# Two hybrid blocks in float32: twenty pairs of projections by seven block products, with accumulating DMAs for weight sums

## Chip, cores and metric

The kernel runs on one core of a Trainium2 chip. The metric is the device time of one execution in microseconds; a faster kernel has a smaller time. All times here are of the kernel before unless the text says otherwise.

## What is computed

Two blocks follow each other on 512 tokens of width 2048, all in float32. Each normalises its input, projects it, mixes tokens in two ways side by side, gates each mix with a silu of a projection, and projects back onto the residual. The first block puts 16 meta tokens in front (528 in all). Cut to what the change touches:

```python
hn = rmsnorm(h, pre_norm_g[layer])                      # 528 x 2048
proj = jnp.einsum('bld,dc->blc', hn, w_in[layer])
qa, ka, va, ga, qb, kb, vb, gb = jnp.split(proj, SPLIT_POINTS, axis=-1)
ya = gqa_axial_mixer(qa, ka, va, ...) * jax.nn.silu(ga)  # 8 heads of 128, 2 key heads
yb = diff_attn_mixer(qb, kb, vb, ...) * jax.nn.silu(gb)  # 8 heads, two softmaxes each
y = jnp.einsum('blc,cd->bld', jnp.concatenate([ya, yb], axis=-1), w_out[layer])
h = h + rmsnorm(y, post_norm_g[layer])
```

The second block (a gated linear recurrence beside stick-breaking attention) stays as it was.

## The kernel before

**Precision.** Every large matmul is done in halves of float32 that TensorE takes at full pace. `split` (L147) makes them: ScalarE copies a tile into its rounded half, and VectorE subtracts that from the original for the rest. Three products (hi-hi, hi-lo, lo-hi; `PASSES`, L282) then give the float32 result, so each block of 128 x 128 weights costs three matmuls per stretch of tokens. The first block's input x, scaled by g1, lies split in `big` for all 16 K tiles; the factor of the row norm is applied to the results.

**Weights.** `_sequence` (L77) lists all weight units in order; each has two halves of 128 x 1024. `load_next` (L257) issues a half's DMA on SP's queue into one of three raw buffers (`wraw`) and splits it into one of three split buffers (`wsp`). `take` (L273) keeps two halves ahead of TensorE.

**Main work.** `main_work` (L931) does the first block's projections in this order: KA, VA, QA0, the A gates (GA 0 to 7), QA1, the B gates (GB 0 to 7), then for each B head QB, KB, VB, then the output projection O1. `fm` (L284) makes one unit of 128 output columns: 16 K tiles x three passes, with the weights stationary and tokens moving. Gates and QB need the 512 real tokens only (one matmul of 512 columns), KB and VB need all 528 (two of 264, half the tokens each, with a load of the weights in front of each). A gate is finished by `silu2` (L430) into `ybuf`; QB, KB, VB into `qs_`, `ks_`, `vs_` in `ar`.

**Side work.** Attention heads are generators beside the main one: `a_scores`, `a_sums`, `b_scores`, `b_values`, `b_sums`. An A head normalises and rotates its queries (`rope`, L444, on VectorE and GpSimd), then for four query tiles makes scores in PSUM (`pss`), their maximum on VectorE (L622), the exponential on ScalarE (L624) and a scaling by the reciprocal sum on VectorE (L627). `pv_steps` (L480) transposes the weights, splits them (`pt`) and multiplies by the values; `gate_y` (L437) multiplies by the gate in `ybuf`. A B head makes two sets of scores per query tile (L684, L687), scales one (L699) and adds them (L700).

**Order.** `run` (L206) is a planner at build time. It keeps a clock of estimated TensorE time, adds a cost for every matmul (`mm`, L178), and takes the first generator whose posted due times (`post`, L188) have come: sides first, main otherwise. The resulting order is fixed on TensorE; the other engines and the DMA queue of SP follow it too, each strictly in its own order.

Of the kernel before, what the change touches and what calls it, by code (L numbers as in the profile page):

```python
# [40 lines left out]

def _units():
# [6 lines left out]
    for name, n in (("KA", 2), ("VA", 2), ("GA", 8), ("QB", 8), ("KB", 8), ("VB", 8), ("GB", 8)):  # L49
        for i in range(n):  # L50
            u[(name, i)] = ("fm", 0, i, cols)
            cols += P
# [23 lines left out]

def _sequence():  # L77
# [19 lines left out]
def hybrid_two_block_kernel(ctx: ExitStack, tc: tile.TileContext, wp, xT, xtok, par, lvec, cst, rg, pg, lruw, out):  # L97
# [34 lines left out]
    def et(n=L):  # L132
        return T([P, L], "e", F32, 5)[:, :n]
# [98 lines left out]
    ybuf = T([P, KT, NTOK], "ybuf")  # L232
    yflat = flat(ybuf)
# [12 lines left out]
    h1d = dram.tile([NTOK, D], F32, tag="h1d", name="h1d")  # L246

# [7 lines left out]
    loaded = []  # L255

    def load_next(n=1024):  # L257
# [4 lines left out]
        raw = T([P, 1024], "wraw", F32, 3)  # L262
        w = T([P, 2, 1024], "wsp", F32R, 3)
# [7 lines left out]
    taken = [0]  # L271

    def take(unit, h):  # L273
# [3 lines left out]
        while len(loaded) < min(len(seq), i + 1 + AHEAD):  # L277
            for _ in load_next():
                pass
        return loaded[i]  # L280

# [15 lines left out]
    def fm_two(units, ps, lag):  # L297

        w = [None, None]
        for i in range(KT + lag):  # L300
            for u, kt in ((0, i), (1, i - lag)):
                if 0 <= kt < KT:
                    if kt % 8 == 0:
                        w[u] = take(units[u], kt // 8)
# [15 lines left out]
    def tm(units, x0, evac, kgs=range(4), toks=range(NT), before_unit=None, after_unit=None, chore=None):  # L320
# [4 lines left out]
        for i, unit in enumerate(units):  # L325
# [5 lines left out]
            if last:  # L331
                ws_ = [take(unit, 0), take(unit, 1)]
# [80 lines left out]
    kvraw = [ar[:, i * L : (i + 1) * L] for i in range(4)]  # L413
# [7 lines left out]
    qs_, ks_, vs_ = ar[:, 4608:5120], ar[:, 5120:5648], ar[:, 2560:3088]  # L421
    osb, osq, orr = ar[:, 3088:3600], ar[:, 3600:4112], ar[:, 1824:2336]
# [18 lines left out]
    def split_y(s):  # L441
        split(big[:, 0, s, :NTOK], big[:, 1, s, :NTOK], ybuf[:, s, :])

# [36 lines left out]
    def pv_steps(h, tag, e, cols, vt, vs, use, extra=()):  # L480

        for hf in range(2):
            yield when("pt", "ptt", (tag, h, 2 * hf))
            hold("pt")
            pt = T([P, 2, 4, 256], "pt", F32R)
# [37 lines left out]
    def side_norms():  # L523
# [3 lines left out]
        for j in range(5):  # L527
# [3 lines left out]
            xs = yflat[:n, (j % 2) * 2048 : (j % 2) * 2048 + 2048]  # L531
            nc.sync.dma_start(xs, xtok[j * P : j * P + n, :])
            act.activation(yflat[:n, 4096:6144], xs, AF.Square, accum_out=ss0[:n, j : j + 1])
# [711 lines left out]
```

## Time and profile before

| | |
|---|---|
| time, three runs | 1728.32, 1728.72, 1729.15 us (median 1728.72) |
| the profiled execution's own time | 1727.61 us |
| its span, first to last instruction | 1725.8 us |
| granted TensorE clock | 1.0 of full speed |
| TensorE busy | 1714.7 us (99%) |
| VectorE, ScalarE, GpSimd busy | 1015.9, 783.8, 91.0 us |
| first gate to last VB, roughly | 107 to 797 us, without QA1 at 229 to 276 |

The profile is of one execution. Its rows name line, engine and operation, then what is written and read. `pj` is the PSUM of the main work, `pss` that of scores, `pmt` and `ptt` that of the sums and transposes; `wraw` and `wsp` are a weight half raw and split, `e` the score tiles, `ar` a shared area of SBUF. L181 is the matmul helper and L149 and L148 are the two steps of `split`, so for these the tile tells which work it is. Matmuls overlap, so the mean of a single one is longer than their spacing.

### The profile page before, as it was taken

The numbers are of one execution on the slowest core, as the hardware profiler recorded it, in microseconds if no ns is written. First come the engines' busy times: TensorE is split into PE (matmuls) and PEld (weight loads), VectorE is DVE, ScalarE is ACT, GpSimd is POOL, SyncE is SP. The second block draws the span as 40 slices with busy tenths as digits, with TensorE's granted clock in tenths as the row PEclk, the third lists the DMA queues.
The fourth block names the chain that finished last, engine by engine and source line by source line (L and its number), as shares of the span: only waits on it lengthen the run. The fifth ranks groups of instructions, "written<-read, shape, count | busy, mean of one in ns | idle before, by whom it ended". The sixth has DMA issues, their size and how long they took to land.

```text
span 1725.8 us, 23791 instructions
## 1 busy us (share of the span) xinstructions
PE 1714.7 (99%) x9496; PEld 1477.6 (86%) x9496; DVE 1015.9 (59%) x1694; ACT 783.8 (45%) x1276; POOL 91.0 (5%) x85
## 2 busy tenths in 40 slices
PE   8999999999999999999999999999999999999998
PEld 8888888889999999988788998888888888888887
DVE  5748634864566666775557869743223664575433
ACT  6434423443445555564445547822223664575311
POOL 0100001100001101000000001100000000010000
PEclk9999999999999999999999999999999999999999
DMA  8321122222221222222567653222222212432223
GB/s 314 121 98 62 63 84 86 68 79 74 76 84 64 72 74 74 74 69 78 171 196 270 218 190 109 92 94 90 98 98 90 81 61 88 153 115 74 86 97 123
DMA packets 53854, 185.81 MB, mean 108 GB/s; under 512 B 6112, under 2 KB 7776, under 8 KB 52064
## 3 DMA queue, kind: packets, MB, share of 16 engines
q1 hardware_dynamic: 53744, 184.30, 32.2%
q8 instruction: 74, 1.21, 0.3%
q14 instruction: 36, 0.29, 0.1%
HBM read 175.89 MB, written 8.39 MB: 107 GB/s over the span
## 4 chain that ended last, share of the span: by engine, by line
PE 96%; DVE 2%; issue 0%; DMA 0%; POOL 0%; ACT 0%; SPq 0%; DVEq 0%; ACTq 0%; POOLq 0%
PE pj L181 84%; PE pmt L181 4%; PE pss L181 4%; PE ptt L184 2%; PE pmt L184 1%; PE bank L181 1%; PE pss L184 1%; DVE wsp L149 0%; DMA wraw<-in_wp 0%; POOL ybuf L450 0%; SPq L374 0%; ACT wsp L148 0%; POOL ar L450 0%; SPq L266 0%; DVE sm L574 0%
## 5 line engine op out<-in xcount | busy, mean ns | idle before, releaser
L181 PE MATMUL pj<-big,wsp 128*128 128x264 f32 (+2 forms) x4608 | 809.0, 332 | 5.9 <-ACT big L375 5.3
L181 PEld LDWEIGHTS pj<-big,wsp 128*128 128x128 f32 x4608 | 688.2, 189 | 86.9 <-ACT big L375 5.6
L181 PE MATMUL pj<-wsp,big 128*128 128x512 f32 x3072 | 736.5, 396 | 0.6 <-DVE big L149 0.6
L181 PEld LDWEIGHTS pj<-wsp,big 128*128 128x128 f32 x3072 | 569.6, 188 | 131.3 <-DVE big L149 0.9
L149 DVE TENSOR_TENSOR wsp<-wraw,wsp 128x1024 fp32r<-128x1024 f32 (+1 forms) x299 | 363.1, 1215 | 387.1 <-ACT wsp L148 386.7
L148 ACT CAST wsp<-wraw 128x1024 fp32r<-128x1024 f32 (+1 forms) x299 | 310.8, 1040 | 496.0 <-PE pj L181 391.6
L148 ACT CAST pt<-ptt 128x512 fp32r<-128x512 f32 (+2 forms) x96 | 50.3, 524 | 76.1 <-PE ptt L184 76.1
L687 ACT ACTIVATE e<-e,sm 128x528 f32<-128x528 f32 x64 | 47.2, 737 | 77.6 <-DVE sm L684 77.1
L149 DVE TENSOR_TENSOR pt<-ptt,pt 128x512 fp32r<-128x512 f32 (+2 forms) x96 | 59.4, 619 | 35.4 <-ACT pt L148 34.7
L181 PEld LDWEIGHTS pmt<-pt,vv 128*128 128x128 f32 x528 | 69.1, 190 | 3.6
L181 PE MATMUL pss<-kk,qq 128*128 128x264 f32 x448 | 71.4, 287 | 0.0
L181 PE MATMUL pmt<-pt,vv 128*128 128x256 f32 (+1 forms) x528 | 69.6, 280 | 0.0
L181 PEld LDWEIGHTS pss<-kk,qq 128*128 128x128 f32 x448 | 63.5, 188 | 3.7
L684 DVE CUSTOM_DVE_ANT_0 e<-pss,ar 128x528 f32<-128x528 f32 x64 | 45.0, 703 | 31.4 <-PE pss L181 30.9
L184 PE MATMUL ptt<-ident,e 128*128 128x128 f32 x336 | 52.6, 273 | 0.1
L184 PEld LDWEIGHTS ptt<-ident,e 128*128 128x128 f32 x336 | 40.6, 140 | 6.9 <-DVE e L627 0.5
L432 DVE TENSOR_TENSOR e<-pj,rbc 128x512 f32<-128x512 f32 x32 | 22.0, 688 | 39.7 <-PE pj L181 39.7
L885 POOL TENSOR_SCALAR_AFFINE_SELECT e<-e 128x128 f32<-128x128 f32 x32 | 15.7, 490 | 476.2 <-ACT e L884 471.1
L654 POOL TENSOR_SCALAR ar<-ar 128x912 f32<-128x912 f32 x8 | 23.4, 2930 | 211.9 <-DVE sm L684 207.4
L624 ACT ACTIVATE e<-pss,sm 128x528 f32<-128x528 f32 x32 | 22.4, 701 | 23.5 <-DVE sm L622 23.4
L450 POOL TENSOR_TENSOR ar<-ar 128x256 f32<-128x256 f32 x16 | 18.4, 1172 | 242.9 <-DVE ar L447 242.9
L894 ACT ACTIVATE e<-e 128x128 f32<-128x128 f32 (+3 forms) x32 | 15.0, 470 | 28.8 <-DVE e L893 28.5
(202 smaller groups left out, 1168.9 us busy)
## 6 DMA issues: line engine op xcount, KB each, us to landing
wraw<-in_wp SPq DMA_DIRECT2D x295, 512.0 KB, 3.5
e<-in_xT SPq DMA_DIRECT2D x16, 264.0 KB, 4.4
ybuf<-in_xtok SPq DMA_DIRECT2D x4, 1024.0 KB, 7.2
ar<-in_xtok SPq DMA_DIRECT2D x4, 1024.0 KB, 5.9
h1d<-ybuf SPq DMA_DIRECT2D x4, 1024.0 KB, 5.4
ybuf<-h1d SPq DMA_DIRECT2D x12, 256.0 KB, 3.6
out<-ybuf SPq DMA_DIRECT2D x12, 256.0 KB, 2.1
ar<-in_pg SPq DMA_DIRECT2D x1, 1024.0 KB, 4.8
```

The source lines that it names most:

```text
L148: act.copy(hi, src)
L149: dve.tensor_tensor(lo, src, f(hi), ALU.subtract)
L181: _queue(nc.tensor.matmul(out, lhsT, rhs, start=start, stop=stop).ins, cost)
L184: _queue(nc.tensor.transpose(out, in_, identity).ins, 110.0)
L432: dve.tensor_tensor(g, g_ps, rb, ALU.mult)
L450: pool.tensor_tensor(v4(blocks(u))[:, :, :, a, :], v4(x)[:, :, :, 1 - a, :], v4(blocks(s))[:, :, :, a, :], ALU.mult)
L624: act.activation(halves(x), sv, AF.Exp, bias=nm, accum_out=l[:, 0:1])
L654: pool.tensor_scalar(bias, dist, 2.0 ** (-(h + 1)), None, op0=ALU.mult)
L684: dve.tensor_tensor_reduce(out=halves(x), in0=s[:, :, :HL], in1=halves(bias[:, b0 : b0 + L]), scale=1.0, scalar=3e38, op0=ALU.add, op1=ALU ...
L687: act.activation(x, x, AF.Exp, scale=-1.0, bias=nm, accum_out=l[:, m : m + 1])
L885: pool.affine_select(z[:, t * P : w], z[:, t * P : w], [[-1, P]], ALU.is_gt, -1e30, base=0, channel_multiplier=1)
L894: act.activation(c, c, AF.Exp)
```

## The change

It touches the 40 units GA, GB, QB, KB, VB of the first block. They are made in 20 pairs (GA with GA, GB with GB, QB with KB of a head, VB of two heads). For the first 12 of the 16 K tiles, a pair is a 2 x 2 block product: two units by two halves of six K tiles, times two halves of six K tiles by two halves of 264 tokens. It is done with seven block products in place of eight; the last four K tiles are done plainly (`rest`) and accumulate into the same four PSUM banks.

- `seven` is a pair's order on TensorE; `produce(p, i)` is the split of the i-th weight operand, called at fixed places, some for the next pair. Operands 1 to 5, 7 and 9 have 768 columns, 6 and 8 (the plain K tiles) 512.
- Of the four sums of weight blocks, the first is done by VectorE (r0 + r1), the other three by DMAs issued on GpSimd that add from DRAM into SBUF (`sum_up`).
- The sums of x blocks are made once (`side_x`); one of them replaces a quarter of `big`.
- `p1s`, `us`, `wv`, `ts` hold parts of the combination, which ScalarE copies or VectorE makes out of PSUM; the `evac_` functions finish the blocks.
- `ybuf` gives its room to the x sums during this stage. So gates are stored to DRAM (`gated`), loaded again before their head's sum, and the results are stored (`yd`) and loaded again before O1 (`fetch_y`). QA1's result goes through DRAM too (`qd`).
- The order becomes KA, VA0, QA0, QA1, VA1, the gate pairs, then QB/KB, VB/VB, QB/KB for two heads at a time. O1's weights aren't prefetched before the last pair is done (`barred`).
- `e` has six buffers instead of five, and the scalings of L627 and L699 go to ScalarE.

The diff, cut to its core (the removed loop over QB, KB, VB and the function `gate` stand in the code above; posts and unchanged uses of renamed areas are left out):

```diff
+def _pairs():
+    pairs = [(("GA", i), ("GA", i + 1)) for i in range(0, 8, 2)] + [(("GB", i), ("GB", i + 1)) for i in range(0, 8, 2)]
+    for h in range(0, 8, 2):
+        pairs += [(("QB", h), ("KB", h)), (("VB", h), ("VB", h + 1)), (("QB", h + 1), ("KB", h + 1))]
+    return pairs
+
...
-    seq = [("VA", 0), ("VA", 1)] + [("QA0", kg) for kg in range(4)]
-    seq += [("GA", i) for i in range(8)] + [("QA1", kg) for kg in range(4)] + [("GB", i) for i in range(8)]
-    for h in range(8):
-        seq += [("QB", h), ("KB", h), ("VB", h)]
+    seq = [("VA", 0)] + [("QA0", kg) for kg in range(4)] + [("QA1", kg) for kg in range(4)] + [("VA", 1)]
...
-        return T([P, L], "e", F32, 5)[:, :n]
+        return T([P, L], "e", F32, 6)[:, :n]
...
+    def load_raw(p, r, slot):
+        if p >= len(PAIRS):
+            return
+        n = WS if r < 4 else NCL * P
+        raw = raw_all[:, WS * slot : WS * slot + n]
+        raw_slot[(p, r)] = slot
+        pair_raw[(p, r)] = raw
+        nc.sync.dma_start(raw, wq[p, r] if r < 4 else wc[p, r - 4])
+    def sum_up(p, r, q):
+        pool.dma_start(pair_raw[(p, r)], wq[p, q], accum_op=ALU.add)
+    def produce(p, i):
+        if p >= len(PAIRS):
+            return
+        r = lambda k: pair_raw[(p, k)]
+        if i == 1:
+            pair_w[(p, "at")] = dict(zip("abcd", w_slots))
+        at = pair_w[(p, "at")]
+        src, place = {1: (0, "a"), 2: (0, "b"), 4: (1, "c"), 5: (3, "d"), 6: (4, "a"), 3: (0, "c"), 8: (5, "d"),
+                      7: (2, "c"), 9: (0, "b")}[i]
+        n = NCL * P if i in (6, 8) else WS
+        slot = at[place]
+        w = halves(wsp_all[:, 2 * WS * slot : 2 * WS * slot + 2 * n])
+        pair_w[(p, i)] = w
+        split(w[:, 0], w[:, 1], r(src))
+        if i == 1:
+            dve.tensor_tensor(r(0), r(0), r(1), ALU.add)
+            sum_up(p, 1, 2)
+        elif i == 2:
+            sum_up(p, 0, 2)
+        elif i == 3:
+            sum_up(p, 0, 3)
+        elif i == 4:
+            load_raw(p, 4, raw_slot[(p, 1)])
+        elif i == 5:
+            load_raw(p, 5, raw_slot[(p, 3)])
+        elif i == 6:
+            w_slots[:] = [at["a"], at["c"], at["d"], at["b"]]
+            load_raw(p + 1, 0, raw_slot[(p, 4)])
+        elif i == 8:
+            load_raw(p + 1, 1, raw_slot[(p, 5)])
+        elif i == 7:
+            load_raw(p + 1, 2, raw_slot[(p, 2)])
+        elif i == 9:
+            load_raw(p + 1, 3, raw_slot[(p, 0)])
...
+    def seven(p, r, c0a, c0b, evac_a1, evac_b, evac_a2, after=None):
+        cs = (c0a, c0b)
+        X1, X2 = slice(0, HL), slice(HL, L)
+        def product(i, bank, x, c, first, last, n=KS):
+            w = pair_w[(p, i)]
+            for j in range(n):
+                for pi, (ws, xs) in enumerate(PASSES):
+                    mm(r[bank][:, c], w[:, ws, j * P : (j + 1) * P], x(xs, j), first and j == 0 and pi == 0,
+                       last and j == n - 1 and pi == 2)
+                yield
+        def rest(i, bank, c0, x1, first, last):
+            w = pair_w[(p, i)]
+            x0 = 0 if x1 else HL
+            for j in range(NCL):
+                for pi, (ws, xs) in enumerate(PASSES):
+                    mm(r[bank][:, c0:HL], w[:, ws, j * P : (j + 1) * P], big[:, xs, 2 * KS + j, x0 + c0 : x0 + HL],
+                       first and j == 0 and pi == 0, last and j == NCL - 1 and pi == 2)
+                yield
+        allc = slice(0, HL)
+        yield from product(1, 0, lambda xs, j: big[:, xs, j, X1], allc, True, True)
+        produce(p, 6)
+        act.copy(p1s[:], r[0][:, :HL])
+        yield from product(4, 2, lambda xs, j: x23[:, xs, j, X2], allc, True, True)
+        produce(p, 3)
+        yield from product(5, 0, lambda xs, j: big[:, xs, KS + j, c0a:HL], slice(c0a, HL), True, False)
+        produce(p, 8)
+        yield from rest(6, 0, c0a, True, False, True)
+        yield from evac_a1()
+        yield from product(3, 1, lambda xs, j: x23[:, xs, j, X1], allc, True, True)
+        produce(p, 7)
+        dve.tensor_tensor(wv[:], r[1][:, :HL], p1s[:], ALU.subtract)
+        dve.tensor_tensor(us[:], r[2][:, :HL], wv[:], ALU.add)
+        yield from rest(6, 3, 0, False, True, False)
+        produce(p + 1, 1)
+        yield from product(2, 0, lambda xs, j: x1s[:, xs, j, :], allc, True, True)
+        produce(p, 9)
+        dve.tensor_tensor(wv[:], r[0][:, :HL], wv[:], ALU.add)
+        dve.tensor_tensor(ts[:], r[0][:, :HL], us[:], ALU.add)
+        yield from product(7, 1, lambda xs, j: big[:, xs, j, HL + c0b : L], slice(c0b, HL), True, False)
+        produce(p + 1, 2)
+        if after:
+            after()
+        yield from rest(8, 2, 0, False, True, True)
+        yield from rest(8, 1, c0b, True, False, True)
+        produce(p + 1, 4)
+        yield from evac_b()
+        yield from product(9, 3, lambda xs, j: big[:, xs, KS + j, X2], allc, False, True)
+        produce(p + 1, 5)
+        yield from evac_a2()
...
+    def fetch_y(s):
+        y = et(NTOK)
+        nc.sync.dma_start(y, yd[s])
+        split(big[:, 0, s, :NTOK], big[:, 1, s, :NTOK], y)
...
+        for j in range(KS):
+            a, b = et(), et()
+            for t, kt in ((a, j), (b, KS + j)):
+                nc.sync.dma_start(t, xT[kt])
+                act.mul(t, t, g1[:, kt : kt + 1])
+            dve.tensor_tensor(b[:, HL:], a[:, HL:], b[:, HL:], ALU.subtract)
+            dve.tensor_tensor(a[:, HL:], a[:, HL:], a[:, :HL], ALU.subtract)
+            dve.tensor_tensor(a[:, :HL], a[:, :HL], b[:, HL:], ALU.subtract)
+            dve.tensor_tensor(s4raw[:, j], b[:, :HL], a[:, :HL], ALU.subtract)
+            split(x23[:, 0, j], x23[:, 1, j], a)
+            split(x1s[:, 0, j], x1s[:, 1, j], b[:, HL:])
+            post(("xs", j), 5000)
+            yield when(("xs", j))
+        post("xs")
+        yield when("x2k1")
+        split(big[:, 0, :KS, HL:], big[:, 1, :KS, HL:], s4raw.whole())
+        post("x4", 4000)
...
-            dve.tensor_scalar(x, x, l[:, 1:2], None, op0=ALU.mult)
+            act.mul(x, x, l[:, 1:2])
...
+            ys[hf] = gin[:, i % 3 * 256 : i % 3 * 256 + 256]
+            nc.sync.dma_start(ys[hf], gated[h][:, hf * 256 : (hf + 1) * 256])
+
+        def use(hf, o):
+            y = ys[hf]
+            dve.scalar_tensor_tensor(y, o, 0.5, y, op0=ALU.mult, op1=ALU.mult)
+            nc.sync.dma_start(yd[h][:, hf * 256 : (hf + 1) * 256], y)
...
-            dve.tensor_scalar(e1, e1, l[:, 3:4], None, op0=ALU.mult)
+            act.mul(e1, e1, l[:, 3:4])
...
+                nc.sync.dma_start(y, gated[8 + h])
...
+        nc.sync.dma_start(yd[8 + h], y)
...
+                        x = et(NTOK)
+                        act.mul(x, accs[t], rnat[:, t : t + 1])
+                        nc.sync.dma_start(qd[t], x)
...
+        def last_x2k1(kt):
+            if kt == KS - 1:
+                post("x2k1")
+            elif kt == 11:
+                for r in range(4):
+                    load_raw(0, r, r)
+                produce(0, 1)
+                produce(0, 4)
+
+        yield from value(1, last_x2k1)
+        produce(0, 2)
+        produce(0, 5)
+        yield when("xs", "x4")
...
+            def silu(g, s):
+                th = et(NTOK)
+                last_tanh[0] = act.activation(th, g, AF.Tanh, scale=0.5).ins
+                dve.scalar_tensor_tensor(g, th, 1.0, g, op0=ALU.add, op1=ALU.mult)
+                nc.sync.dma_start(gated[s], g)
+                post(("gate", s), 4500)
+            def evac_a1():
+                ga[0] = et(NTOK)
+                dve.tensor_tensor(ga[0][:, :HR], r0[:, NM:HL], p1s[:, NM:], ALU.add)
+                return ()
+            def evac_b():
+                g = et(NTOK)
+                dve.tensor_tensor(g[:, :HR], r1[:, NM:HL], wv[:, NM:], ALU.add)
+                dve.tensor_tensor(g[:, HR:], r2_[:, :HL], ts[:], ALU.add)
+                dve.tensor_tensor(g, g, rbq, ALU.mult)
+                silu(g, slot + 1)
+                return ()
+            def evac_a2():
+                g = ga[0]
+                dve.tensor_tensor(g[:, HR:], r3[:, :HL], us[:], ALU.subtract)
+                dve.tensor_tensor(g, g, rbq, ALU.mult)
+                silu(g, slot)
...
+        def qkb(h):
+            def evac_a1():
+                if h:
+                    yield when(("qkused", h - 1))
+                dve.tensor_tensor(qs_[:, :HR], r0[:, NM:HL], p1s[:, NM:], ALU.add)
+            def evac_b():
+                dve.tensor_tensor(ks_[:, :HL], r1[:, :HL], wv[:], ALU.add)
+                dve.tensor_tensor(ks_[:, HL:], r2_[:, :HL], ts[:], ALU.add)
+                dve.tensor_tensor(ks_, ks_, rbc, ALU.mult)
+                return ()
+            def evac_a2():
+                dve.tensor_tensor(qs_[:, HR:], r3[:, :HL], us[:], ALU.subtract)
+                dve.scalar_tensor_tensor(qs_, qs_, -0.125, rbq, op0=ALU.mult, op1=ALU.mult)
...
+        for h in range(0, 8, 2):
+            yield from qkb(h)
+            yield from vvb(h)
+            yield from qkb(h + 1)
+        barred[0] = len(seq)
```

More of the change, by code (lines that the diff above doesn't have):

```diff
@@ L255, in hybrid_two_block_kernel @@
     loaded = []
+    raw_all = T([P, 3072], "wraw")
+    wsp_all = T([P, 6144], "wsp", F32R)
     def load_next(n=1024):
@@ L261, in load_next @@
         unit, h = seq[len(loaded)]
-        raw = T([P, 1024], "wraw", F32, 3)
-        w = T([P, 2, 1024], "wsp", F32R, 3)
+        i = len(loaded) % 3
+        raw = raw_all[:, 1024 * i : 1024 * (i + 1)]
+        w = halves(wsp_all[:, 2048 * i : 2048 * (i + 1)])
         loaded.append(w)
@@ L276, in take @@
         taken[0] = i + 1
-        while len(loaded) < min(len(seq), i + 1 + AHEAD):
+        while len(loaded) < min(barred[0], i + 1 + ahead):
             for _ in load_next():
@@ L478, in v_tiles, with pv_steps @@
         return vt, vs
-    def pv_steps(h, tag, e, cols, vt, vs, use, extra=()):
+    def pv_steps(h, tag, e, cols, vt, vs, use, extra=(), before=None):
         for hf in range(2):
@@ new lines, in main_work, with gates @@
+        yield from value(1, last_x2k1)
+        produce(0, 2)
+        produce(0, 5)
+        yield when("xs", "x4")
+        ta, tb = pjt(), pjt()
+        banks = (ta[:, 0], ta[:, 1], tb[:, 0], tb[:, 1])
+        r0, r1, r2_, r3 = banks
+        HR = HL - NM
+        pair_no = {pair: i for i, pair in enumerate(PAIRS)}
+        last_tanh = [None]
+        def gates(name, i):
+            slot = i + (8 if name == "GB" else 0)
+            ga, gb = [None], [None]
+            def silu(g, s):
[21 more added lines that the diff above has]
+                return ()
+            yield from seven(pair_no[((name, i), (name, i + 1))], banks, NM, NM, evac_a1, evac_b, evac_a2)
@@ L965, in main_work @@
+        for name in ("GA", "GB"):
+            for i in range(0, 8, 2):
+                yield from gates(name, i)
+        with tc.issue_after(last_tanh[0]):
             lnload[0] = act.preload_act_table_set("natural_log_exp_and_others").ins
+        ysplit = set()
         def split_ready(kt):
```

187 lines of the change are left out of this document (127 added, 60 removed).

## The prediction

> **What bounds the kernel now.** I read the page first: busy times, the granted clock, the chain that ended last.
>
> ```profile
> span 1725.8 us, 23791 instructions
> PE 1714.7 (99%) x9496; PEld 1477.6 (86%) x9496; DVE 1015.9 (59%) x1694; ACT 783.8 (45%) x1276; POOL 91.0 (5%) x85
> PEclk9999999999999999999999999999999999999999
> PE 96%; DVE 2%; issue 0%; DMA 0%; POOL 0%; ACT 0%; SPq 0%; DVEq 0%; ACTq 0%; POOLq 0%
> PE pj L181 84%; PE pmt L181 4%; PE pss L181 4%; PE ptt L184 2%; PE pmt L184 1%; PE bank L181 1%; PE pss L184 1%; DVE wsp L149 0%; DMA wraw<-in_wp 0%; POOL ybuf L450 0%; SPq L374 0%; ACT wsp L148 0%; POOL ar L450 0%; SPq L266 0%; DVE sm L574 0%
> ```
>
> TensorE is the bound: 99% busy at full clock, 96% of the chain. So matmul time removed is time saved, as long as nothing makes TensorE wait. TensorE takes its instructions in the planner's fixed order, so a late weight split or evacuation stops it at once. The second limit is therefore VectorE, and 59% is only its mean. For that I asked for windows inside the stage with gates and A heads (312 to 352 us) and the stage with B heads, alone and by tile. The columns are length, then PE, PEld, DVE, ACT and POOL busy with counts.
>
> ```profile
> 312.00:352.00 40.00, 40.00 (x233) 34.69 (x232) 34.36 (x78) 19.49 (x39) 7.13 (x5) 1.00 0.20 65
> 572.00:710.00 138.00, 138.00 (x992) 129.94 (x991) 94.51 (x177) 71.94 (x139) 13.68 (x6) 1.00 0.21 70
> 710.00:756.00 46.00, 46.00 (x332) 43.29 (x330) 39.27 (x71) 31.01 (x60) 2.48 (x2) 1.00 0.24 75
> ```
>
> VectorE reaches 34.36/40 = 86% and 39.27/46 = 85% there, and TensorE doesn't lose a microsecond. So 86% is hidden; no window of this trace shows what happens above it.
>
> **What the matmuls save.** Uninterrupted stretches of the chain give the pace of each width: 512 columns, 264 (both halves of one K tile), and 256 with a weight load each.
>
> ```profile
> 237.39 56.31 PE pj L181 x242
> 456.64 4.64 PE pj L181 x38
> 985.90 44.83 PE pj L181 x377
> ```
>
> 512 columns cost 56.31/242 = 0.2327 us, 264 cost 4.64/38 = 0.1221. The third row, 0.1189 for 256, is the nearest to the new products, where each matmul has its own weights; scaled to 264 it gives 0.1226, so that costs nothing extra. I take 0.1221, and 0.1147 for 248.
>
> Removed: 16 gates and 8 QB of 48 matmuls at 512 (1152 x 0.2327 = 268.1) and 16 KB and VB of 96 at 264 (1536 x 0.1221 = 187.5), together 455.6 us. Added: 20 pairs of 7 x 18 + 4 x 12 = 174. Those that start behind the 16 meta tokens are 248 wide: 60 of a gate pair's, 30 of a QB/KB pair's, none of a VB pair's. So 2760 x 0.1221 + 720 x 0.1147 = 337.0 + 82.6 = 419.6 us. **Saved: 36.0 us** (34.3 at 0.1226). A pair takes 20.8 us (gates), 21.0 (QB/KB), 21.2 (VB). The second block, QA, KA, VA and O1 keep their matmuls.
>
> **What VectorE and ScalarE must do for it.** Rows by form, over the whole run except the second fence, which is of 312 to 352 us.
>
> ```profile
> L149 DVE TENSOR_TENSOR wsp<-wraw,wsp 128x1024 fp32r<-128x1024 f32 x295 | 361.4, 1226 | 386.2 <-ACT wsp L148 385.8
> L148 ACT CAST wsp<-wraw 128x1024 fp32r<-128x1024 f32 x295 | 309.2, 1048 | 494.6 <-PE pj L181 391.6 <-issue 85.1 <-DMA wraw<-in_wp 12.4
> L624 ACT ACTIVATE e<-pss,sm 128x528 f32<-128x528 f32 x32 | 22.4, 701 | 23.5 <-DVE sm L622 23.4
> L149 DVE TENSOR_TENSOR big<-ybuf,big 128x512 fp32r<-128x512 f32 x32 | 21.2, 682 | 6.6 <-ACT big L148 6.5
> L148 ACT CAST big<-ybuf 128x512 fp32r<-128x512 f32 x32 | 19.0, 616 | 13.3 <-PE pj L181 10.4 <-DVE ybuf L439 1.6 <-DVE ybuf L732 1.1
> L699 DVE TENSOR_SCALAR e<-e,sm 128x528 f32<-128x528 f32 x32 | 15.8, 493 | 0.8
> L439 DVE SCALAR_TENSOR_TENSOR ybuf<-pmt,ybuf 128x256 f32<-128x256 f32 x32 | 13.4, 417 | 11.4 <-PE pmt L181 11.4
> ```
> ```profile
> L627 DVE TENSOR_SCALAR e<-e,sm 128x528 f32<-128x528 f32 x7 | 3.5, 494 | 0.2
> L448 DVE TENSOR_TENSOR ar<-ar 128x512 f32<-128x512 f32 x2 | 2.1, 1074 | 0.0
> L432 DVE TENSOR_TENSOR e<-pj,rbc 128x512 f32<-128x512 f32 x3 | 2.1, 688 | 0.8 <-PE pj L181 0.8
> L434 DVE SCALAR_TENSOR_TENSOR ybuf<-e 128x512 f32<-128x512 f32 x3 | 2.0, 683 | 0.0
> L447 DVE TENSOR_TENSOR ar<-ar,sm 128x512 f32<-128x512 f32 x2 | 1.4, 692 | 0.1
> ```
>
> A 768-wide split lies between the 512 and 1024 rows: VectorE 0.95, ScalarE 0.83. A gate pair on VectorE: seven splits of 768 and two of 512 (8.05), the sum r0 + r1 (0.95), four combinations of 264 with PSUM (0.43 each, 1.7), four quarter evacuations (1.7), two products with rbq (0.69) and two last steps (0.68): **15.1 us**. Before it was 4 x 1.226 + 2 x (0.688 + 0.683) = 7.6. The other pairs take 8.05 + 0.95 + 1.7 + 1.7 + 1.4 = 13.8.
>
> The two windows, rebuilt with the new pairs in the old mix, need the share that is main work:
>
> ```profile
> 312.00:352.00 40.00, 28.00 (x114) 20.35 (x113) 2.06 (x3) 0.00 (x0) 1.00 0.20 65
> 312.00:352.00 40.00, 28.00 (x114) 20.35 (x113) 6.48 (x5) 5.25 (x5) 1.00 0.20 65
> 312.00:352.00 40.00, 6.59 (x42) 5.75 (x42) 4.19 (x6) 4.77 (x13) 1.00 0.20 65
> 572.00:710.00 138.00, 116.42 (x737) 101.20 (x735) 6.28 (x9) 0.00 (x0) 1.00 0.21 70
> 572.00:710.00 138.00, 116.42 (x737) 101.20 (x735) 22.75 (x19) 19.89 (x19) 1.00 0.21 70
> ```
>
> (The first and fourth row are by tile pj, the second and fifth wsp, the third pss.) Gates and A heads: 114 matmuls of 512 are 26.5 us, in which 26.5/20.8 = 1.27 pairs fit, 19.2 us of VectorE. The heads' part is 34.36 - 6.48 - 4.1 (L432, L434) = 23.8, less seven scalings that go to ScalarE (3.5): 20.3. Sum 39.5 of 40 us; with the rope of every head, of which L448 shows 2 in 1.75 heads, nothing is missing. B heads: 144 matmuls of 512 and 593 of 264 (three QB, and KB and VB) are 105.9 us, 5.03 pairs, 69.4 us of VectorE; the heads' part 94.51 - 22.75 - 6.28 = 65.5, less 12 scalings (5.9): 59.6. Sum 129.0 of 138 us. **VectorE goes from 86% to 99% and from 68% to 93%.** ScalarE in the first window: heads 19.49 - 5.25 - 1.8 (three tanh at the 616 row) = 12.4, seven scalings at the L624 price 4.9, 1.27 pairs 11.0 (each nine splits 7.0, one copy and two tanh 1.7 by the 512 row), sum 28.3 of 40; it isn't the bound.
>
> What the new second limit costs goes by how full VectorE can be kept. The scores row (42 matmuls, 7 scores in 40 us) makes 22.9 us a head, 183 us for eight A heads: 4.6 such windows. Eight B heads take 8 x 46 - 24 saved, 344 us: 2.5 windows. At 98% full: A (40.3 - 40) x 4.6 = 1.4 us, B nothing. At 95%: A 1.6 x 4.6 = 7.4, B nothing. At 90%: A 3.9 x 4.6 = 17.9, B 5.3 x 2.5 = 13.3. At 86%, the fullest that the trace shows: A 27, B 30. I take 93%, midway between the shown 86% and full: A 2.5 x 4.6 = **11.5**, B 0.7 x 2.5 = **1.8**. More isn't likely, because weights now come just in time: a split is asked for one or two products (some 3.5 us) before its use, not two units.
>
> **The ends and the queues.** DMA issues, KB and us to landing:
>
> ```profile
> wraw<-in_wp SPq DMA_DIRECT2D x295, 512.0 KB, 3.5
> ybuf<-in_xtok SPq DMA_DIRECT2D x4, 1024.0 KB, 7.2
> ```
>
> The first pair's weights are loaded at VA1's tile 11, 24 matmuls (2.9 us) before its end. Its second product, number 4, needs the load (3.5), split 1 (1.8), the sum (0.95), the accumulating DMA and split 4 (1.8). No row has an accumulating DMA; below is the plain 512 KB at 3.5, above the 7.2 of 1024 KB, since it reads two operands of 384 KB. I take 3.5, nearest in size: 11.6 us, needed at 2.9 + 2.2: **6.5 us** idle (10.2 at the upper end). At O1 the weights share the pairs' buffers, so the first split waits for the last product: 1.05 + 1.23, **2.3 us** (0 if B heads fill it, 5.8 if the load is late too). In between, sum and split of number 4 have products 2, 7, 8, 8, 9, 1 (11.7 us) for 8.0 us of work: 3.7 us spare. The page DMA: Bandwidth & Descriptors of the Trainium skill (Anatomy of one DMA) fits 2.0 us + bytes/436e3 to DMAs from GpSimd; for 384 KB I estimate 2.9 us from it, with which the start would idle 5.9 us; no run here shows one.
>
> The sixteen gate stores, the loads before each PV, the y stores and reloads (about 60 DMAs of 128 to 256 KB) stand in SP's queue between weight loads: each waits for a VectorE result, and weight loads wait behind it. They hide while a pair's loads have some 5 us in hand; bounds 0 and 5 us, I take **3**. The x sums of side_x (six times four of 264 and splits of 528 and 264, 17 us of VectorE by the rows above) lie beside QA1, which keeps VectorE a quarter busy (third and fourth number: PEld and DVE):
>
> ```profile
> 229.00:276.00 47.00, 47.00 (x213) 38.32 (x212) 11.30 (x13) 11.27 (x14) 0.00 (x0) 1.00 0.24 79
> ```
>
> They cost nothing there; ahead of a busy VectorE they would cost up to 17. The sixth e buffer: nothing, or a small gain.
>
> **Sum.** The profiled execution took 1727.6 us (span 1725.8, 1.8 around it): 1727.6 - 36.0 + 11.5 + 1.8 + 6.5 + 2.3 + 3 = 1716.7. The median of the three runs is 1.1 above that execution: **1718 us**.
>
> **Rivals.**
> 1. *VectorE's lag is hidden in full* (fill 98%, start covered by heads' work): 1728.7 - 36.0 + 1.4 + 0 to 9 = 1694 to 1703. For it: the 86% windows with TensorE at 40.00 of 40. Against: just-in-time splits.
> 2. *VectorE's order takes TensorE's place as the bound, slower.* ScalarE's copies wait in order for accumulating DMAs, VectorE's subtractions wait for the copies, and VectorE with 99% to do can't catch up. At 86% fill: 27 + 30 + 12 = 69, that is 1762; at 88%: 22 + 21 + 12 = 55, 1748. It decides at about 91%, where A (15.6), B (9.4) and the ends (12) eat the 36. For it: nothing here ran above 86%; every pair has nine splits at fixed places. Against: a VectorE with a backlog finds its inputs ready.
> 3. *The accumulating DMA is late.* From 7.2 us (3.5 + 3.7 spare) each microsecond costs one per pair, 20 in all. VectorE catches up meanwhile, so its 13.3 falls away: 1705 + 20 for each; at 8.4 us the gain is gone, at 9.0 it is 1741. L448 takes 1074 ns beside GpSimd against 692 for L447, so the two do hinder each other. The Trainium skill, SBUF — State Buffer (Who interferes with whom), speaks against this change: while VectorE runs a two-port fast mode, GpSimd can't write descriptors, and it names 620 ns alone against some 3100 beside such an operation. The L627 and L699 rows, the likeliest such, leave for ScalarE here, and 2.5 us more is still inside the spare; I therefore give it little.
> 4. *Gain and loss meet*: fill 90.5 to 91.7%, 1725 to 1732.
>
> **Chances.** Forecast (fill 92 to 97%, 1708 to 1724) 0.45; rival 1 0.13; rival 4 0.13; rival 2 0.21; rival 3 0.08. A change under 0.2% (3.5 us) can't be told from none here. Faster 0.45 + 0.13 = 0.58, same 0.13, slower 0.29. The range, 1697 to 1744, leaves out the last of rival 1 and the outer half of rivals 2 and 3.
>
> **What would show it.** TensorE's pj matmuls fewer by 36 us; idle time of TensorE in front of 264-wide matmuls, released by VectorE's wsp, most of it while A heads run beside gates, where VectorE stands above 90%; 6 us before the first pair's second product and 2 before O1. Wrong would be: TensorE idle behind DMAs into wraw in every pair (rival 3), idle time spread over the B heads (rival 2), or none (rival 1).

## The result and the profile after

The changed kernel takes 1901.62 us (median of four runs, 1893.17 to 1904.35) against 1728.76 us before: 1.0992 times the time before, 95% interval 1.0955 to 1.1028. The prediction was 1718 us, with a range up to 1744. It is wrong in sign and far outside its range.

The page of the kernel after, with the lines that answer to those of before (the chain's first line among them):

```profile
span 1901.9 us, 26572 instructions
PE 1740.8 (92%) x10288; PEld 1543.1 (81%) x10288; DVE 1139.2 (60%) x1947; ACT 902.5 (47%) x1485; POOL 136.6 (7%) x145
PEclk9999989899999899989998999999999999999999
PE 52%; DVE 1%; issue 0%; ACT 0%; DMA 0%; DVEq 0%; ACTq 0%; SPq 0%
```

The span grew by 176.1 us. TensorE was idle for 11.1 us before (1725.8 - 1714.7) and for 161.1 now (1901.9 - 1740.8): 150.0 of the 176.1 are idle time. The other 26.1 are busy time, although there are 36.0 us fewer matmuls by the prediction's count. The granted clock explains that: its mean over the run is 1.000 before and 0.967 after, and (1714.7 - 36.0) / 0.967 = 1736, close to the 1740.8 shown. VectorE at 60% isn't the bound; between 200 and 1000 us, where the pairs run, it is busy 522 of 800 us (65%):

```profile
200.00:1000.00 800.00, 667.37 (x4787) 635.96 (x4785) 522.29 (x992) 401.25 (x744) 93.87 (x82) 0.93 0.43 110
```

So neither engine is full there, which points to waits. The waits of TensorE in the kernel after, in us, times, longest:

```profile
PE pj L196 <- DVE xmisc L466: 37.1, 16, 4.1
PE pj L196 <- DVE xmisc L460: 30.5, 20, 3.6
PE pj L196 <- DVE e L1217: 15.5, 7, 6.1
PE pj L196 <- DVE ar L1254: 9.4, 6, 2.3
PE pj L196 <- ACT big L163: 8.7, 1, 8.7
PE pj L196 <- DVE ar L1280: 7.8, 4, 3.8
PE pss L199 <- ACT e L1162: 6.4, 1, 6.4
PE pj L196 <- DVE wsp L164: 5.9, 3, 4.9
```

`wsp`, the split weights, which the prediction expected here, has 5.9 us. At the top stand VectorE's reads of the pair's PSUM banks: L460 makes `us` out of r2, L466 makes `ts` out of r0, and L1217, L1254 and L1280 are the three `evac_a1`, which read r0. Together 100.3 us. One such place in the order of time (start, length, engine, line, what; in brackets the idle time before it and its releaser):

```profile
282.39 0.93 PE L196 MATMUL pj<-big,wsp 128*128 128x248 f32 x6
286.11 0.68 DVE L798 TENSOR_REDUCE sm<-ar 128x4 f32<-128x512 f32 x1
287.52 0.41 DVE L1217 TENSOR_TENSOR e<-pj,xmisc 128x248 f32<-128x248 f32 x1
288.08 1.84 PE L196 MATMUL pj<-x,wsp 128*128 128x264 f32 x9 [4.76 <-DVE sm L174]
```

The last row is product 3 (the one with operand `x23` behind `evac_a1`), and it writes r1. TensorE stands still for 4.76 us until L1217 has read r0, which VectorE does late because it is in a rope's chain (L798 and the small steps after it). The releaser that the row names, L174, is only the next small step: L1217 ends at 287.93. Product 3 doesn't touch r0. But `banks = (ta[:, 0], ta[:, 1], tb[:, 0], tb[:, 1])`: r0 and r1 are the two banks of one PSUM tile, r2 and r3 of the other. Read this way, every product that follows a read of its tile's other bank waits for that read, six times in a pair, and `seven` puts each of these reads right in front of such a product: r0 is read and product 3 goes to r1 (L1217), r2 is read and `rest(6)` goes to r3 (L460), r0 is read and product 7 goes to r1 (L466), and so on. The first run takes the sharing away.

### The profile page after: what moved, and what is told of

It is laid out like the page before. It is cut to its first block, busy times and chain, and to the rows that moved or that the text cites. A ratio compares the mean times of both kernels' runs of the same rounds, so it can differ in the third digit from the quotient of the medians.

```text
span 1901.9 us, 26572 instructions
## 1 busy us (share of the span) xinstructions
PE 1740.8 (92%) x10288; PEld 1543.1 (81%) x10288; DVE 1139.2 (60%) x1947; ACT 902.5 (47%) x1485; POOL 136.6 (7%) x145
## 4 chain that ended last, share of the span: by engine, by line
PE 52%; DVE 1%; issue 0%; ACT 0%; DMA 0%; DVEq 0%; ACTq 0%; SPq 0%
PE pj L196 47%; PE pmt L196 1%; PE pss L196 1%; PE bank L196 1%; PE ptt L199 1%; PE pmt L199 0%; PE pss L199 0%; DMA yd<-xmisc 0%; DMA e<-yd 0%; DVE big L164 0%; ACT wsp L163 0%; DVE wsp L164 0%; DVE e L164 0%; DVE e L898 0%; ACT e L901 0%
## 5 line engine op out<-in xcount | busy, mean ns | idle before, releaser
L196 PE MATMUL pj<-big,wsp 128*128 128x264 f32 (+3 forms) x4320 | 662.3, 312 | 86.6 <-DVE xmisc L466 37.1
L196 PEld LDWEIGHTS pj<-big,wsp 128*128 128x128 f32 x4320 | 603.4, 196 | 132.6 <-DVE xmisc L460 35.1
L164 DVE TENSOR_TENSOR wsp<-wraw,wsp 128x1024 fp32r<-128x1024 f32 (+3 forms) x399 | 426.4, 1070 | 408.3 <-ACT wsp L163 400.6
L163 ACT CAST wsp<-wraw 128x1024 fp32r<-128x1024 f32 (+3 forms) x399 | 367.9, 924 | 554.0 <-PE pj L196 467.4
L196 PE MATMUL pj<-x,wsp 128*128 128x264 f32 x720 | 112.8, 308 | 40.8 <-DVE e L1217 15.5
L196 PEld LDWEIGHTS pj<-x,wsp 128*128 128x128 f32 x720 | 102.6, 208 | 44.6 <-issue 31.1
L349 POOL DMA_DIRECT2D wraw<-in_wq x60 | 52.8, 880 | 531.0 <-DVE wsp L164 224.2
L196 PE MATMUL pss<-kk,qq 128*128 128x264 f32 x448 | 75.8, 299 | 3.2 <-DVE sm L898 3.2
L196 PE MATMUL pj<-x1s,wsp 128*128 128x264 f32 x360 | 53.7, 297 | 0.0
L196 PEld LDWEIGHTS pj<-x1s,wsp 128*128 128x128 f32 x360 | 49.6, 201 | 0.2
```

What stands on the lines that cost most here:

```text
L163: act.copy(hi, src)
L164: dve.tensor_tensor(lo, src, f(hi), ALU.subtract)
L196: _queue(nc.tensor.matmul(out, lhsT, rhs, start=start, stop=stop).ins, cost)
L349: pool.dma_start(pair_raw[(p, r)], wq[p, q], accum_op=ALU.add)
```

## Experiments

The first four runs ask whether the shared tiles are the cause, against two rivals of the prediction, a VectorE that is too full and a late accumulating DMA.

**Four tiles of one bank.** The same four banks, each a tile of its own; the copies of K and V out of two banks are made in two instructions.

```diff
-    psj = ... tile_pool(name="psj", bufs=2, ...)
+    psj = ... tile_pool(name="psj", bufs=4, ...)
+    class Banks:
+        def __init__(self):
+            self.b = [psj.tile([P, 512], F32, tag="pj", name="pj") for _ in range(2)]
-        return psj.tile([P, 2, 512], F32, tag="pj", name="pj")
+        return Banks()
```

> The changed kernel with each of its four PSUM banks as a tile of its own (four tiles of 512 columns instead of two of 2 x 512); KA and VA are copied out in two instructions instead of one. Theory A (a product waits for VectorE's reading of the other bank of the same tile, six times a pair, because waits are kept per tile): TensorE's idle time falls from 161 us to under 40, its mean clock rises from 0.967 to 0.99 or more, and the time falls to 1705 to 1735 us. Theory B (VectorE is behind its work, so every result of it is late): idle time moves to the weight splits, the time stays above 1850 us. Theory C (the accumulating DMAs are late): the time stays above 1850 us, with TensorE waiting for splits that wait for DMAs.

Measured: 1758.31 us, 1.0181 of before (1.0164 to 1.0198). 143 of the 173 us are gone, with no instruction of the pairs changed and with all 10288 matmuls in the same order on TensorE, by the tiles that each one writes and reads. A line of the page, and the head of the list of waits:

```profile
PE 1692.8 (96%) x10288; PEld 1504.6 (86%) x10288; DVE 1134.8 (65%) x1947; ACT 898.2 (51%) x1489; POOL 135.3 (8%) x145
```
```profile
PE pj L208 <- ACT big L175: 10.2, 1, 10.2
PE ptt L211 <- DVE pt L176: 10.0, 4, 3.0
PE pj L208 <- DVE wsp L176: 6.3, 4, 5.3
PE pss L211 <- ACT e L141: 6.1, 1, 6.1
PE pj L208 <- ACT xmisc L462: 5.9, 7, 2.0
PE pj L208 <- ACT big L549: 5.4, 1, 5.4
PE pss L208 <- DVE sm L910: 5.3, 3, 3.1
```

All waits of products for `us`, `ts` and the evacuations have left the list: none of them was needed. A product still fills one bank while VectorE reads another, so the wait was the program's, kept for a tile as a whole. TensorE does 36 us fewer matmuls at a mean clock of 0.991: 1678.7 / 0.991 = 1694, shown 1692.8. Its idle time is 62.3 us (1755.1 - 1692.8). The clock is as theory A said, but the idle time was to be under 40 us and the expected range was missed by some 23 us above, so something else costs too.

**Two of the four.** Only r0 and r1 have tiles of their own; r2 and r3 still share one (the pool gives one-bank and two-bank tiles in turn).

> As the run with four tiles, but banks r2 and r3 still share one tile of 2 x 512; r0 and r1 are tiles of their own. Theory A: three of six false waits per pair are left, so about half of the loss comes back: 1790 to 1830 us. Theories B and C: no change against the changed kernel, 1880 to 1905 us.

Measured: 1824.47 us, 1.0552 (1.0536 to 1.0568), about half of the way. What is left at the top of the waits is the read of r2 ahead of the product into r3:

```profile
PE pj L211 <- DVE xmisc L475: 46.7, 20, 5.1
```

L475 is `us`, the L460 of the kernel after: 20 waits, one a pair. The waits for `ts` and for `evac_a1`, which read r0, are gone, and the smaller ones for VectorE's reads of PSUM that are left (13.3 us together) are all for reads of r2 and r3. That singles out the sharing itself.

**The kernel before with four tiles.** The same edit in the kernel before.

> The kernel before with one tile for each PSUM bank, and KA, VA, KB, VB taken out of PSUM in two instructions instead of one. Theory A: before, both banks of a tile are read together after the last matmul and the next unit goes to the other tile, so nothing was lost there: within 0.3% of 1728.7 us. Theories B and C say the same, a little more for the 20 added VectorE instructions of some 0.4 us.

Measured: 1727.7 us, 0.9999 (0.999 to 1.0008). Four tiles give nothing by themselves; before, each unit filled its tile and went on in the other.

**Short sums.** The 60 accumulating DMAs add only 64 of 768 columns, so the weight sums are incomplete.

```diff
-        pool.dma_start(pair_raw[(p, r)], wq[p, q], accum_op=ALU.add)
+        pool.dma_start(pair_raw[(p, r)][:, :64], wq[p, q, :, :64], accum_op=ALU.add)
```

> The changed kernel, with each accumulating DMA adding only 64 of its 768 columns (so the weight sums are partial): a twelfth of the bytes, with the same number of DMAs and waits. Theory C (late accumulating DMAs stall the splits): under 1800 us. Theories A and B: within 1% of the changed kernel, 1885 to 1910 us.

Measured: 1900.31 us (1896.68 to 1903.94), the kernel after took 1901.62. The waits stay, L466 at 37.0 and L460 at 30.2. The accumulating DMA isn't the cause of the loss in the kernel after.

The runs that follow ask what keeps the four tiles 40 us above the 1718 predicted. All of these kernels have four tiles.

**Two shortcuts at O1.** The last head's result is split from SBUF instead of being stored to `yd` and loaded back, and O1's first three weight loads are issued when the last pair has split its last raw block.

```diff
+        if s == 15:
+            y = last_y[0]
...
+            if p == len(PAIRS) - 1:
+                for k in range(len(loaded), len(loaded) + 3):
+                    sent.add(k)
+                    unit, h = seq[k]
+                    nc.sync.dma_start(raw_all[:, 1024 * (k % 3) : 1024 * (k % 3 + 1)], wp[UIDX[unit], h])
```

> Four one-bank tiles, and two shortcuts at the passage to the output projection: the last head's gated result goes to the operand from SBUF instead of through DRAM and back, and the first three loads of the output projection's weights are issued when the last pair has split its last raw block, not when the first product asks for them. Theory A (what is left of the loss with four tiles is a list of separate late arrivals, each to be cured where it stands): the 10.2 us wait of the product for ScalarE's split of the last operand shrinks by the DRAM round trip (3.8 + 2.6 us in the four-tile run, so about 6), the 5.3 us wait for the first weights by the load (3.5), 1758 - 9.5 = 1748, 1745 to 1753. Rival B (VectorE and ScalarE are full in the pair stages, and a wait that is taken away only shows up again at the next product): no change, 1756 to 1761.

Measured: 1751.19 us, 1.0129 (1.0114 to 1.0144), 7 us less. The wait that it shortens, in the kernel with four tiles:

```profile
851.36 0.33 SPq L965 DMA_DIRECT2D yd<-xmisc  x1
855.20 0.33 SPq L621 DMA_DIRECT2D e<-yd  x1
857.82 0.62 ACT L175 CAST big<-e 128x512 fp32r<-128x512 f32 x1 [10.20 <-DMA e<-yd]
858.49 0.80 PE L208 MATMUL pj<-wsp,big 128*128 128x512 f32 x1 [10.23 <-ACT big L175]
```

Store, load and split in a row: 3.8 + 2.6 us of DRAM ahead of the split. It falls from 10.2 to 3.8 us.

**Later due times.** The planner puts a step of the attention on TensorE when it takes VectorE's part to be done. Here it counts on later ends, and `p1s` is copied ahead of a split:

```diff
-                post("ptt", 3300)
+                post("ptt", 5000)
-            post("pss", 3800)
+            post("pss", 5300)
-            post("pmt", 3200)
+            post("pmt", 4200)
-            post("p", 4300)
+            post("p", 5300)
-            post(("kv", 2 + i), 1000)
+            post(("kv", 2 + i), 7000 if i else 1000)
-        produce(p, 6)
         act.copy(p1s[:], r[0][:, :HL])
+        produce(p, 6)
```

> Four one-bank tiles; the copy of the first product goes ahead of a split on ScalarE, and the planner counts on later ends of VectorE's and ScalarE's work: 1.0 to 1.7 us more for the attention steps, 6 us more for the last V block of the first stage, so the order on TensorE puts more projection products ahead of them. Theory A: most of the waits for pt (10.0), for the score minimum (5.3), for ptail (3.2), for the last V block (6.1) and for the copied first product (5.9) go, 30.5 us in the four-tile run, and the clock with them: 1758 - 22 to - 38 = 1720 to 1736. Rival B (VectorE is the bound of the attention stages; it is 75 to 84 percent busy in their 50 us stretches): the same time is lost in other products, 1750 to 1765.

Measured: 1787.5 us, 1.0342 (1.0325 to 1.036), 29 us more, and both theories missed. The wait for `pt` fell from 10.0 to 2.6 us, but a new one came on top:

```profile
PE ptt L211 <- DVE e L926: 17.2, 10, 4.8
```

L926 is the last step of a B head's scores. The planner now takes every score step to end 1.5 us later, and the scores come too late for the sum behind them. It fits an attention chain without slack; the run moves five due times and a copy at once and doesn't tell them apart.

**Both sets.** The two edits together.

> Four tiles with both sets of edits. Theory A: the gains add, 1710 to 1728, level with the kernel before or under it; the fewer matmuls show at last. Rival B: 1745 to 1765.

Measured: 1777.68 us, 1.0291 (1.0275 to 1.0306): 9.8 us under the later due times alone, and above both ranges. The shortcuts keep their gain, the due times their loss.

**Scalings back.** The two `act.mul` of the softmax go back to VectorE.

> Four tiles, with the two softmax scalings back on VectorE: 64 instructions of about 0.7 us move from ScalarE, 42 us over the two attention stages (700 us), which takes VectorE there from about 80 to 86 percent. If VectorE's lag is what the attention steps wait for, the waits for pt and the score minimum grow and the run takes 1764 to 1785; if ScalarE's queue was the late one (the copied first product, the splits), the time stays or falls, 1748 to 1760.

Measured: 1751.88 us, 1.0134 (1.0119 to 1.0149): 6 us less, although VectorE has more to do (1156.8 us for 1134.8). The wait for the copied first product falls from 5.9 to 2.4 us. In this kernel a little work off ScalarE is worth more than off VectorE; it fits that `p1s` and the first half of every split stand in ScalarE's queue.

**The cures together.** Both shortcuts, the scalings back, `p1s` ahead of the split, the last V block counted 6 us later.

> Four one-bank tiles with the edits that the runs before point to: the two shortcuts at the output projection (7 us in the run of their own), the two scalings back on VectorE (6 us), the copy of the first product ahead of a split on ScalarE, and the last V block of the first stage counted 6 us later by the planner (in the run with later due times TensorE did 4.3 us more work between 150 and 200 us). No other due time is raised. If these losses are separate and add: 1758 - 7 - 6 - 4 - 2 = 1739, 1733 to 1744. If one only takes the other's place: 1748 to 1752.

Measured: 1740.13 us, 1.0068 (1.0053 to 1.0083), as the sum of the parts said. No other kernel with whole sums was faster, and it is still 12 us above before. In the profiled spans these 12 are 31.1 us more idle time (42.2 for 11.1) and 17.4 us lost to the clock (1696.1 - 1678.7), less the 36.0 of matmuls. VectorE in its two fullest stretches of 100 us:

```profile
500.00:600.00 100.00, 95.58 (x772) 94.33 (x771) 90.23 (x176) 61.03 (x121) 17.78 (x14) 0.98 0.53 126
600.00:700.00 100.00, 94.94 (x754) 93.70 (x754) 88.28 (x171) 60.45 (x118) 19.56 (x15) 0.95 0.49 116
```

**Low halves on GpSimd.** Of each pair but the first, two low halves and the sum of two raw blocks leave VectorE.

```diff
+        if i in (1, 2) and p:
+            act.copy(w[:, 0], r(src))
+            pool.tensor_tensor(w[:, 1], r(src), f(w[:, 0]), ALU.subtract)
...
-            dve.tensor_tensor(r(0), r(0), r(1), ALU.add)
+            (pool if p else dve).tensor_tensor(r(0), r(0), r(1), ALU.add)
```

> The kernel with the cures, and of each pair but the first the low halves of two weight operands (the first and second product's) and the sum of the first two raw blocks go from VectorE to GpSimd: three of VectorE's 0.9 us instructions a pair, 19 pairs, about 50 us of its 545 us or so in the pair stages. If VectorE's fill is what is left (the waits for pt, for the score minimum): 1722 to 1733 where the cures give 1739. If what is left is the length of chains and their due times, no change within 3 us; if GpSimd is late with the operands, or holds up VectorE, slower by 5 or more, with waits for wsp.

Measured: 1766.86 us, 1.0218 (1.0201 to 1.0235), 27 us more than the cures. VectorE was to lose some 50 us and lost 17 (1141.3 for 1158.1): other instructions of it got longer, the scaled sum of L939 (there L943) from 764 to 939 ns. Most waits for VectorE's steps grew a little, those for `wsp`, which the last theory named, only from 2.0 to 4.2 us.

**The cures with short sums.** Incomplete sums again.

> The kernel with the cures, its 60 accumulating DMAs adding 64 of 768 columns each, so that the sums are incomplete. The critical chain of the four-tile run holds wraw for some 3 percent of the span. If the accumulating DMA (4.9 us from issue to landing) decides somewhere once the false waits are gone: 5 us or more under the kernel with the cures. If it always lands in time: within 3 us of it.

Measured: 1733.77 us, 1.003 (1.0019 to 1.004), 6.4 us less. With the false waits gone the accumulating DMA does cost something. Half of it is at the first pair, where TensorE is busy 48.96 us for 45.70 (the cures, then with short sums):

```profile
150.00:200.00 50.00, 45.70 (x356) 44.82 (x355) 29.33 (x46) 23.05 (x38) 5.39 (x6) 0.93 0.61 146
150.00:200.00 50.00, 48.96 (x409) 48.59 (x408) 35.68 (x62) 25.37 (x41) 6.26 (x7) 1.00 0.42 113
```

**One due time.** Only `post("ptt")` of the A heads, 5000 for 3300.

> The kernel with the cures, and one due time alone raised: in the first attention stage the second transposes of a half are counted 1.7 us later behind the split of the first (5.0 for 3.3 us). There TensorE waits 7.4 us for VectorE's split in the run with the cures, four times. If those waits are lost time that other products can fill: 1740 - 6 = 1734, 1731 to 1737. If the later step only pushes the chain behind it, as it did when all due times were raised: 1740 or more.

Measured: 1751.15 us, 1.0127 (1.011 to 1.0144), 11 us more, on the side of the second theory (1740 or more). The waits for `pt` are gone, and those for `p1s` go from 3.6 to 16.3 us. The longest of them (ScalarE's queue in order):

```profile
225.16 0.62 ACT L175 CAST wsp<-wraw 128x512 fp32r<-128x512 f32 x1 [6.68 <-DMA wraw<-in_wc]
226.21 0.36 ACT L469 COPY xmisc<-pj 128x264 f32<-128x264 f32 x1
226.62 1.21 PE L208 MATMUL pj<-big,wsp 128*128 128x248 f32 x4 [6.51 <-ACT xmisc L469]
```

ScalarE waits 6.68 us for a load, and the copy that product 5 needs stands behind that split. The load had stood in SyncE's queue behind a gate load. Four more kernels ask whether that queue is the cause: gate loads (`dma_start` of `gated` ahead of each sum) go to GpSimd, and in two of them the stores to `yd` as well.

> The kernel with the cures; the loads of the gates ahead of each weighted sum (16 + 8) are issued on GpSimd instead of SyncE, where weight loads stood behind them. If SyncE's queue is part of what is left: 1740 - 3 to - 10 = 1730 to 1737. If GpSimd's own queue is delayed by them (it issues the accumulating DMAs and does a part of the rope): 1742 to 1755. If neither matters: within 2 us of 1740.

> The same, and the stores of the gated results (yd) on GpSimd too: no transfer that waits for VectorE but the gate stores is left ahead of weight loads on SyncE. If SyncE's queue is part of what is left: 1726 to 1736. If GpSimd's queue becomes the late one: 1742 to 1760.

> The kernel with the cures and the one raised due time (1751), with the gate loads on GpSimd. If its 11 us came from weight loads held in SyncE's queue behind the gate loads: 1732 to 1738, the waits for the copied first product (16.3 us) mostly gone. If the longer attention chain itself is the cause: 1748 to 1753.

> The raised due time with gate loads and result stores on GpSimd: by the queue theory 1728 to 1736, by the chain theory 1748 to 1755.

Measured, beside 1740.13 and 1751.15: 1741.27, 1744.15, 1748.33 and 1748.07 us. The queue theory falls; it explains 3 of the 11 us at most, and the last two times are those that the chain theory named. In the third the wait for `p1s` is still 13.9 us. The 1744.15 can't be told from the cures, since the runs of the two overlap. Why the later step of the A heads brings so much lateness to ScalarE's queue is left open, and so is what would bring the last 12 us.

## Why the prediction was wrong

- **The step that failed is the sum's list of waits.** Within the pairs it let a product wait for its weights (`wsp`) and priced the rest as VectorE's fill. It has no term for a product that waits until another bank of its tile is read: that wait stood at nothing without a reason, though the changed kernel has `banks` as halves of two tiles and a read in front of each such product, and though the prediction's first part says that a late evacuation stops TensorE at once. Shown: four tiles take away 143 of the 173 us, two of the four about half, the short sums none. The waits also lowered the clock: 161 us of idle time at 0.967, 103 at 0.974 (two of four tiles), 62 at 0.991 (four tiles), 11 at 1.000 before.
- **What the matmuls save** (36.0): right, as far as a mean clock can tell. With it, 1692.8 x 0.991 = 1677.6 us of TensorE with four tiles, 37.1 under before.
- **VectorE at 99% and 93%**, of which 13.3 us of loss followed: the model was wrong more than the size. The fill came out at 65% with false waits, 81% with four tiles (463.40 of 575 us), and 88 to 90% in the two fullest stretches of 100 us with the cures, with TensorE 95% busy beside it. Nor does a nearly full VectorE have to stop TensorE. With the cures there is a stretch in which VectorE is busy 98% and TensorE loses 0.3 us:

```profile
175.00:750.00 575.00, 547.86 (x4477) 540.61 (x4476) 463.40 (x896) 348.44 (x649) 88.07 (x81) 0.99 0.55 135
520.00:540.00 20.00, 19.68 (x163) 19.41 (x162) 19.65 (x39) 14.07 (x28) 4.65 (x3) 1.00 0.65 154
```

  What was lost with four tiles is single late steps (pt 10.0, the score minimum 5.3, ptail 3.2), 18.5 us; due times that hide them lose more elsewhere. Rival 2 named the right loser, products that wait for VectorE, with a wrong mechanism: VectorE was far from full.
- **Start of the first pair** (6.5): the size is met by luck. There are 6.1 to 6.4 us of idle time, but in front of the last V block's transposes, which wait for ScalarE's copy, not in front of the second product. In the kernel after:

```profile
163.63 1.33 PE L199 MATMUL pss<-ident,e 128*128 128x128 f32 x5 [6.39 <-ACT e L1162]
```

- **O1** (2.3): 15.5 us with four tiles (10.2 and 5.3). The sum has no term for the last head's round trip through DRAM (10.2); the 5.3 is the split of the first weights. Its two halves take the 1.05 and 1.2 us of the prediction, but VectorE's began 2.8 us after ScalarE's had ended (755.97 for 753.18), behind other work in VectorE's queue.
- **SyncE's queue** (3): small, as assumed; with the gate loads taken out of it, the kernel with the cures takes 1741.27 for 1740.13 us.
- **The accumulating DMA**: 4.9 us to landing where 3.5 was taken; plain loads of the same size take 3.2:

```profile
wraw<-in_wq SPq DMA_DIRECT2D x80, 384.0 KB, 3.2
wraw<-in_wq POOLq DMA_DIRECT2D x60, 384.0 KB, 4.9
L349 POOL DMA_DIRECT2D wraw<-in_wq x60 | 52.8, 880 | 531.0 <-DVE wsp L164 224.2
```

  4.9 is inside the 7.2 from which rival 3 was to decide; what it costs is the 6.4 us of the cures with short sums. The 2.9 us estimated from the Trainium skill (DMA: Bandwidth & Descriptors, Anatomy of one DMA) was too low for a transfer that adds. The Trainium skill's rule on GpSimd's descriptor writes beside VectorE's fast modes (SBUF — State Buffer, Who interferes with whom) doesn't show: with the scalings back on VectorE, seven of the 60 issues ran beside one of them; they took 863 to 929 ns and landed in 4.7 to 5.9 us, where all 60 took 853 to 1043 ns and landed in 4.6 to 6.6.
- **The clock** had no term: at 0.991 it costs 1692.8 - 1678.7 = 14 us with four tiles.

From the profiled span of before, 1725.8, the four-tile kernel adds up thus: -36.0 of matmuls, +18.5 single steps of VectorE, +6.1 start, +15.5 O1, +5.9 `p1s`, +14 clock, and +4.8 for smaller waits (6.1, less the 1.3 of before): 29 us, and its span is 29 above.

## What to carry to other kernels

Before you price an engine's fill, list for each product every wait that its output has, the other parts of its tile included: where two PSUM banks are filled and read in turn, give each a tile of its own. When an engine is less than 70% busy and another still waits for it, look at the order and the latency of single steps, not at sums of busy time. Idle gaps on TensorE cost more than their length when the clock falls behind them: here 1.3 times (four tiles: 51.2 us more idle, 14.1 lost to the clock) to 1.4 times (the kernel after: 150.0 and 62.1). So a change that saves 2% of the matmuls and adds a gap of a microsecond to each product loses.

## What the runs showed of the hardware

The granted clock falls at a single gap. In the kernel with the cures, the stretches of 20 us around its longest gap inside the pairs (3.64 us at 663.59):

```profile
640.00:660.00 20.00, 19.95 (x165) 19.66 (x163) 18.83 (x36) 12.86 (x26) 3.08 (x3) 1.00 0.46 109
660.00:680.00 20.00, 14.99 (x96) 14.54 (x97) 15.32 (x33) 11.00 (x22) 3.82 (x2) 0.74 0.34 86
680.00:700.00 20.00, 20.00 (x167) 19.87 (x166) 17.99 (x34) 12.31 (x26) 4.43 (x4) 1.00 0.54 117
```

A mean of 0.74 over 20 us is 10.2 us at a clock of 0.50, as the trace's own record of the clock has it. 2.8 us of these are idle, so some 3.7 us of matmul time is lost, beside 5.0 us of idle time. The Trainium skill gives gaps above some 3.4 us as those behind which the clock drops (TensorE: Matmul & The Clock Gate, HAM oscillation — how this bites in real kernels). The row above agrees with it, but the kernel after doesn't. Its trace has 26 stretches at 0.50 within the run, of 3.4, 6.8, 10.2 or 13.7 us, 122.9 us together, and only nine gaps above 3.4 us. Of its 23 gaps of 2.0 to 3.4 us, 17 have such a stretch beginning inside them or within 3.4 us behind them; a single gap of 2.12 us at 872.9 was enough. Of the 34 gaps of 0.5 to 1.5 us, one has. So gaps from about 2 us count here.

VectorE and GpSimd hinder each other on plain float32 sums in SBUF: three of VectorE's instructions a pair moved to GpSimd (57 of 0.95 us) took 17 us off VectorE, not 54, and on GpSimd they take 1.9 to 2.0 us each.
